# mLSTM's gate rows: loaded as rows and spread over the partitions by TensorE

## The chip, the cores and the metric

One Trainium2 chip, one of its cores. The metric is device microseconds of one execution of the whole program: two layers of a hybrid block, from the input in HBM to the normed output in HBM. The time of a kernel is the median of its runs.

## What is computed

The input has 2048 latent tokens and 256 context tokens of width 1024. Each layer projects the modulated, normed tokens to the inputs of four head groups (differential attention, HGRN2, windowed attention, mLSTM) and a gate, runs the groups, joins their outputs, and projects them back. The change lies in the mLSTM, a gated linear recurrence that runs forwards and backwards over time:

```python
logd = jnp.where(tri, cum[..., :, None] - cum[..., None, :] + ig[..., None, :], -jnp.inf)
inter = cum + m0[..., None]
m_t = jnp.maximum(jnp.max(logd, axis=-1), inter)
dmat = jnp.exp(logd - m_t[..., None])
g0 = jnp.exp(inter - m_t)
s = jnp.einsum('bhnld,bhnsd->bhnls', q, k) * dmat
num = (jnp.einsum('bhnls,bhnsv->bhnlv', s, v)
       + g0[..., None] * jnp.einsum('bhnlk,bhnkv->bhnlv', q, c0))
den = jnp.sum(s, axis=-1) + g0 * jnp.einsum('bhnlk,bhnk->bhnl', q, n0)
hid = num / jnp.maximum(jnp.abs(den), jnp.exp(-m_t))[..., None]
```

`dmat` is the causal matrix of decays of a chunk, `g0` the weight of the state that the chunk starts from. Both depend, up to a term per key, on one number per query: these are the gate rows. Four heads of width 64 each, two directions.

## The kernel before

The kernel is written in a tile framework: pools of named buffers, semaphores and the order of an engine's instructions come from its scheduler, which follows the order of the program text as far as it finds the instructions ready. Each layer has these stages. The layer's input is normed and transposed; its projections run on PE as f16 products with a high and a low part; the differential attention runs woven with the rest of the projections; then windowed attention (`swa_stream`), mLSTM (`mlstm_stream`), HGRN (`hgrn_stream`) and the output projection with the residual (`out_stream`) are woven together. They work on tiles of 128 tokens, 18 in layer 0 (16 of latent tokens and 2 of context) and 16 in layer 1, 34 in all; HGRN takes two tiles at a time.

The weave is a Python loop over generators. A stream yields its place (in tiles) and a spacing; the loop resumes the ready stream that is furthest behind. Ready is measured in PE time that the helper `mm` (the product, L94) adds up by a formula in `pe_ns`: the columns of a product, times four for f32, over 2.4 GHz. Constants in ORDER_X and ORDER_Y set the spacings. In the first phase, until the projections are through, the first tiles of windowed attention and mLSTM run beside `rest_stream`, which hands out the projections; in the second phase HGRN and the output projection join.

Helpers record the operations: L94 `mm`, L101 `tp` (transpose on PE), L105 `act` (ScalarE, ACT), L108 `tt` (tensor_tensor on VectorE, DVE, or GpSimd, POOL), L111 `stt` (DVE). Transfers are issued mostly from SyncE (SP), in program order.

Names that the change touches:

- `dr1` and `dg0`: the gate rows in HBM, per direction and tile 4 heads x 128 queries in f32, written earlier in the layer.
- `mlm`: two causal masks, 128 x 128 each, 0 or -1e30, f32. `swm`: the masks of the windowed attention and the identity, in bf16; its last part is `identb`.
- `mlstm_load(i)`: the loads of tile i. `qt`, `kt` (queries and keys), `v1` (values with a column of ones), `r1b` (the row of dr1, for two directions and four heads, repeated on all 128 partitions by a broadcast transfer, L1383), `g0b` (the rows of dg0, repeated on 64 partitions for each head of a pair, L1385), `og` (output gate, L1388). In the same function POOL multiplies g0b with qt and adds the mask to r1b, ACT takes the Exp of r1b with a bias per key (TM), DVE clamps og (L1394) and ACT takes its sigmoid. r1b, g0b and the other tiles have two buffers.
- `mlstm_stream`: at the start of tile i it calls mlstm_load(i + 1), then makes the products qk (`mqk`), DVE multiplies them onto r1b, and after a yield it makes, for each direction, `num` from g0b times the state (`cst`) and r1b times v1, with a yield after each direction.
- `bank`: hands out the PSUM banks of the tag "gp" in a ring of three, four in the second phase, to mqk, num, HGRN's gA and go, and the output's ft.

Other names in the rows: E and QQ are HGRN's decay factors and scaled queries, cm and lk their loads, yt the tile that collects the four groups' outputs, fx the output product, ph and swt the windowed attention's weights before and after a transposing transfer, ptm and pfm the projections, modps the product that makes the modulation of the layers.

Of the kernel before, what the change touches and what calls it, by code (L numbers as in the profile page):

```python
# [10 lines left out]
F32 = mybir.dt.float32  # L11
F16 = mybir.dt.float16
BF16 = mybir.dt.bfloat16
U8 = mybir.dt.uint8
AF = mybir.ActivationFunctionType
ALU = mybir.AluOpType
# [17 lines left out]
P = 128  # L34
# [19 lines left out]
M_ID, M_HG, M_SWP, M_SWN, M_MLF, M_MLB, NMASK = 0, 1, 8, 9, 10, 11, 12  # L54
# [10 lines left out]
def bc(ap, axis, n):  # L65

    a = ap.unsqueeze(axis)
    shape = list(a.shape)
    shape[axis] = n
    return a.broadcast_to(shape)  # L70
# [3 lines left out]
def kernel(  # L74
# [8 lines left out]
    V, A, G, PE, SP = nc.vector, nc.scalar, nc.gpsimd, nc.tensor, nc.sync  # L83
# [9 lines left out]
    def mm(o, lhsT, rhs, start, stop):  # L93
        PE.matmul(o, lhsT=lhsT, rhs=rhs, start=start, stop=stop)  # L94
        n = 1
        for d_ in rhs.shape[1:]:
            n *= d_
        pe_ns[0] += max(128, n * 4 if rhs.dtype == F32 else n) / 2.4
# [5 lines left out]
    def act(o, i, f, **kw):  # L104
        A.activation(out=o, in_=i, func=f, **kw)  # L105

    def tt(e, o, a, b, op):
        return e.tensor_tensor(out=o, in0=a, in1=b, op=op)  # L108
# [5 lines left out]
    ident = const.tile([P, P], F32, tag="ident", name="ident")  # L114
# [35 lines left out]
    sel = const.tile([P, 2], F32, tag="sel", name="sel")  # L150
# [108 lines left out]
    for l in range(n_layers):  # L259
# [11 lines left out]
        def dt_(name, shape, dt=F32):  # L271
            return dram.tile(shape, dt, tag=f"{name}{l}", name=f"{name}{l}")
# [16 lines left out]
        dr1 = dt_("dr1", [2, NT, 4, P])  # L289
        dg0 = dt_("dg0", [2, NT, 4, P])  # L290
        dog = dt_("dog", [T, 256])
# [6 lines left out]
        TM = lp.tile([P, 3, 2, NT * 4], F32, tag="TM", name=f"TM{l}")  # L298
# [3 lines left out]
        def jpos(d, t):  # L302

            return (t - NL if t >= NL else t + 2) if d == 0 else NT - 1 - t
# [896 lines left out]
        with ExitStack() as st4:  # L1201
            sw = st4.enter_context(tc.tile_pool(name=f"sw{l}", bufs=2, reuse_waits="tile", side="right"))
            ml = st4.enter_context(tc.tile_pool(name=f"ml{l}", bufs=2, reuse_waits="tile", side="right"))
# [9 lines left out]
            def bank(shape, name):  # L1213
                turn_[0] += 1
                if gps2 and turn_[0] % GPB == 0:
                    return gps2.tile(shape, F32, tag="gp", name=name)
                return gps.tile(shape, F32, tag="gp", name=name, bufs=GPB - 1)
# [10 lines left out]
            def room(i):  # L1228

                return lambda: i < done["out"] + (YTB if done["rest"] else 2)  # L1230
# [25 lines left out]


            mv = masks.rearrange("p (m q) -> p m q", q=P)
            mlm = ml.tile([P, 2, P], F32, tag="mlm", name="mlm", bufs=1)
            SP.dma_start(mlm, mv[:, M_MLF:M_MLF + 2])  # L1260
            swl = sw.tile([P, 640], F32, tag="sp", name="swl")[:, 0:3 * P].rearrange("p (m q) -> p m q", q=P)
            SP.dma_start(swl[:, 0:2], mv[:, M_SWP:M_SWP + 2])
            V.tensor_copy(swl[:, 2], ident)
            swm = sw.tile([P, 3, P], BF16, tag="swm", name="swm", bufs=1)
            V.tensor_copy(swm, swl)
            identb = swm[:, 2]


            KSc = sw.tile([P, 4, CTX], F16, tag="KSc", name="KSc", bufs=1)
# [98 lines left out]
            def mlstm_load(i):  # L1368
                if i >= len(order):
                    return None  # L1370
                t = order[i]
                qt_ = ml.tile([P, 2, P], F32, tag="qt", name="qt")
                SP.dma_start(qt_, dmq[:, :, t * P:(t + 1) * P].rearrange("b p t -> p b t"))
                kt_ = ml.tile([P, 2, P], F32, tag="kt", name="kt")
                SP.dma_start(kt_, dmk[:, :, t * P:(t + 1) * P].rearrange("b p t -> p b t"))
                v1 = ml.tile([P, 4, 65], F32, tag="v1", name="v1")
                SP.dma_start(v1[:, :, 0:64], dmv[t * P:(t + 1) * P].rearrange("p (h d) -> p h d", h=4))
                G.memset(v1[:, :, 64:65], 1.0)
                js = [jpos(d, t) for d in range(2)]
                r1b = ml.tile([P, 2, 4, P], F32, tag="r1b", name="r1b")  # L1380
                g0b = ml.tile([P, 2, 2, P], F32, tag="g0b", name="g0b")
                for d in range(2):
                    SP.dma_start(r1b[:, d], dr1[d, js[d]].partition_broadcast(P))  # L1383
                    for a in range(2):
                        SP.dma_start(g0b[a * 64:(a + 1) * 64, d],  # L1385
                                     dg0[d, js[d]].rearrange("(a i) q -> i a q", i=2)[a].partition_broadcast(64))
                og = ml.tile([P, 256], F32, tag="og", name="og")
                SP.dma_start(og, dog[t * P:(t + 1) * P])  # L1388
                tt(G, g0b, g0b, bc(qt_, 1, 2), ALU.mult)
                for d in range(2):  # L1390
                    tt(G, r1b[:, d], r1b[:, d], bc(mlm[:, d], 1, 4), ALU.add)
                    for h in range(4):
                        act(r1b[:, d, h], r1b[:, d, h], AF.Exp, bias=TM[:, 0, d, js[d] * 4 + h:js[d] * 4 + h + 1])
                V.tensor_scalar(og, og, ZLOW, None, ALU.max)  # L1394
                sigmoid(og, og)
                return js, qt_, kt_, v1, r1b, g0b, og

            def mlstm_stream():
                places = state_places(ml, 65, 1, "cst")
                nxt = mlstm_load(0)  # L1400
                for i in range(len(order)):
                    yield i, 0.0 if i else SW0, room(i)
                    js, qt_, kt_, v1, r1b, g0b, og = nxt
                    nxt = mlstm_load(i + 1)
                    cst = states_of(dmC, [order[i]], 65, places, i)
                    hq = yt_of(i)[:, 768:].rearrange("p (h d) -> p h d", d=64)
                    qks = [bank([P, 2, P], "mqk") for _ in range(2)]
                    for pr in range(2):
                        for pa_ in range(2):
                            r_ = slice(pa_ * 64, pa_ * 64 + 64)  # L1410
                            mm(qks[pa_][:, pr], kt_[r_, pr], qt_[r_, pr], True, True)
                    for pa_ in range(2):
                        dv = r1b.rearrange("p d (a i) q -> p d a i q", i=2)[:, :, :, pa_]
                        tt(V, dv, bc(qks[pa_], 1, 2), dv, ALU.mult)
                    yield i + 0.2, MLW, None
                    for d in range(2):
                        num = bank([P, 2, 2, 65], "mnum")
                        dn = ml.tile([P, 4], F32, tag="dn", name="dn", bufs=4)
                        for pr in range(2):
                            mm(num[:, pr].rearrange("p i c -> p (i c)"), g0b[:, d, pr], cst[:, d, pr, 0], True, False)  # L1420
                            for pa_ in range(2):
                                h = pr * 2 + pa_
                                mm(num[:, pr, pa_], r1b[:, d, h], v1[:, h], False, pa_ == 1)
                        nv = num.rearrange("p a i c -> p (a i) c")
                        act(dn, nv[:, :, 64], AF.Abs)
                        tt(V, dn, dn, TM[:, 2, d, js[d] * 4:js[d] * 4 + 4], ALU.max)
                        V.reciprocal(dn, dn)
                        hd = ml.tile([P, 4, 64], F32, tag="hd", name="hd", bufs=1) if d else hq
                        tt(V, hd, nv[:, :, 0:64], bc(dn, 2, 64), ALU.mult)
                        yield i + 0.5 + 0.4 * d, MLW, None  # L1430
                    tt(G, hq, hq, hd, ALU.add)
                    sq = ml.tile([P, 64], F32, tag="msq", name="msq", bufs=1)
                    rs = ml.tile([P, 2, 4], F32, tag="mrs", name="mrs")
                    for j in range(4):
                        act(sq, hq[:, j], AF.Square, accum_out=rs[:, 0, j:j + 1])
                    rstd_of(rs[:, 1], rs[:, 0], 64)
                    tt(V, hq, hq, bc(rs[:, 1], 2, 64), ALU.mult)
                    tt(G, hq, hq, bc(gml, 1, 4), ALU.mult)
                    hqf = hq.rearrange("p h d -> p (h d)")
                    tt(G, hqf, hqf, og, ALU.mult)  # L1440
                    done["ml"] = i + 1
# [292 lines left out]
```

## Time and profile before

| | |
|---|---|
| median of 3 runs | 4094.21 us (4089.32 to 4104.06) |
| profiled execution | 4102.18 us |
| its span, first to last instruction | 4100.4 us |
| PE busy | 3358.2 us (82%) |
| DVE busy | 2831.4 us (69%) |
| ACT busy | 2330.9 us (57%) |
| POOL busy | 2375.0 us (58%) |
| DMA, mean | 152 GB/s |

The profile is one execution. An engine is busy while one of its instructions runs; PE's ends are modelled. Idle time of an engine is put down to what ended it: "A <- B" is A waiting for B. The chain is followed back from the last instruction, at each step to what released it, or to the instruction before it on its engine. "SPq" is time in which SP issues transfers.

### The profile page before, as it was taken

How to read it: one execution, taken by the hardware profiler on the slowest of the kernel's cores; microseconds unless marked ns; L12 is line 12 of the kernel's file. 1: busy time of each engine (PE TensorE's matmuls, PEld its weight loads, DVE VectorE, ACT ScalarE, POOL GpSimd, SP SyncE). 2: the span in 40 equal slices, each digit the busy share in tenths (PEclk: the TensorE clock that was granted, in tenths of full speed). 3: DMA queues.
4: the chain of work that ended last, by engine and by line, in shares of the span. 5: the costliest groups of instructions: out<-in, count | busy, mean ns of one | idle time of the engine just before them, and what ended most of it. 6: DMA issues, size and time to landing. Idle time of an engine off the chain costs nothing. (4 is left out here: it accounts for less than half of the span.)

```text
span 4100.4 us, 77666 instructions
## 1 busy us (share of the span) xinstructions
PE 3358.2 (82%) x29798; PEld 2269.8 (55%) x29798; DVE 2831.4 (69%) x4343; ACT 2330.9 (57%) x4662; POOL 2375.0 (58%) x1701
## 2 busy tenths in 40 slices
PE   6988878888768996888888988778887698758888
PEld 4656645444546765555557466444445476545554
DVE  5158888888896647465544398988888865467665
ACT  4245655556655636566654266656666665456764
POOL 4443455443445538798966535665334564488885
PEclk8999989999989995898889999999998899869999
DMA  6356866667656628577845457667676584366783
GB/s 211 91 149 150 186 136 159 140 141 154 145 128 157 161 95 200 149 194 185 205 119 177 126 125 151 135 140 155 148 162 142 125 193 116 106 162 170 183 194 104
DMA packets 1267259, 622.12 MB, mean 152 GB/s; under 512 B 931972, under 2 KB 1214152, under 8 KB 1266888
## 3 DMA queue, kind: packets, MB, share of 16 engines
q1 hardware_dynamic: 1164520, 490.65, 53.1%
q10 hardware_dynamic: 102368, 126.52, 9.2%
q8 instruction: 234, 3.83, 0.4%
q14 instruction: 137, 1.12, 0.1%
HBM read 291.76 MB, written 131.23 MB: 103 GB/s over the span
## 5 line engine op out<-in xcount | busy, mean ns | idle before, releaser
L108 POOL TENSOR_TENSOR p<-p,p 128x1024 f16<-128x1024 f32 (+2 forms) x264 | 629.4, 2385 | 792.7 <-ACT p L1084 722.8
L105 ACT ACTIVATE p<-scr,sm 128x1024 f32<-128x1024 f32 (+2 forms) x528 | 628.3, 1194 | 417.8 <-DVE sm L1073 145.2
L94 PE MATMUL ptm<-wb,hh 128*128 128x256 f16 (+2 forms) x5024 | 835.6, 273 | 32.6 <-DVE dSs L111 7.9
L1048 DVE TENSOR_REDUCE sm<-scr 128x1 f32<-128x1024 f32 (+2 forms) x528 | 699.3, 1327 | 218.3 <-PE scr L94 214.5
L94 PE MATMUL pfm<-hh,wb 128*128 128x512 f16 (+1 forms) x2592 | 805.7, 375 | 32.7 <-DVE gz L111 10.1
L94 PE MATMUL ptm<-wb,hl 128*128 128x256 f16 (+2 forms) x2512 | 672.1, 273 | 1.7 <-POOL hl L108 1.7
L94 PEld LDWEIGHTS <-wb 128*128 128x128 f16 x3888 | 378.1, 101 | 414.3 <-issue 84.0
L94 PE MATMUL scr<-Ks,Qs 128*128 128x512 f16 (+1 forms) x1296 | 364.8, 381 | 284.5 <-ACT p L105 279.4
L94 PEld LDWEIGHTS <-hh 128*128 128x128 f16 x5024 | 480.1, 100 | 133.9 <-issue 40.0
L94 PE MATMUL pfm<-hl,wb 128*128 128x512 f16 (+1 forms) x1296 | 485.6, 375 | 0.0
L111 DVE SCALAR_TENSOR_TENSOR p<-p,sm,p 128x1024 f32<-128x1024 f32 (+2 forms) x264 | 413.8, 1568 | 8.1
L94 PEld LDWEIGHTS <-Qs 128*128 128x128 f16 x1296 | 130.7, 102 | 425.2 <-issue 354.5
L94 PE MATMUL fx<-wo,mh 128*128 128x512 f16 x1088 | 342.4, 396 | 16.8 <-DVE xt L111 8.5
L1084 ACT CAST p<-p 128x1024 f16<-128x1024 f32 (+2 forms) x264 | 297.7, 1128 | 39.2 <-DVE p L111 33.8
L94 PEld LDWEIGHTS <-wt 128*128 128x128 f16 x4640 | 243.9, 102 | 71.4 <-DMA wt<-p 24.4
L94 PE MATMUL pv<-Vs,wt 128*128 128x128 f16 (+1 forms) x4640 | 258.5, 213 | 21.9 <-DMA wt<-p 13.5
L94 PEld LDWEIGHTS <-hl 128*128 128x128 f16 x2512 | 250.8, 100 | 35.4 <-POOL hl L108 3.4
L108 POOL TENSOR_TENSOR ph<-swp,ph 128x640 f16<-128x640 f32 (+2 forms) x136 | 196.0, 1442 | 53.7 <-ACT ph L1335 44.3
L108 POOL TENSOR_TENSOR E<-lk,cm 128x512 f32<-128x512 f32 (+1 forms) x136 | 204.8, 1506 | 34.6 <-DMA cm<-dhc 17.8
L94 PE MATMUL fx<-wo,mlo 128*128 128x512 f16 x544 | 212.9, 391 | 1.4 <-DVE mlo L108 1.1
L105 ACT ACTIVATE E<-E 128x1024 f32<-128x1024 f32 x136 | 143.2, 1054 | 102.8 <-POOL E L108 98.9
L108 DVE TENSOR_TENSOR QQ<-hq,E 128x512 f32<-128x512 f32 x119 | 143.8, 1214 | 65.2 <-ACT E L105 46.7
(301 smaller groups left out, 6577.2 us busy)
## 6 DMA issues: line engine op xcount, KB each, us to landing
wraw<-in_w_in_dram SPq DMA_DIRECT2D x60, 512.0 KB
dgt<-ga ACTq DMA_DIRECT2D x68, 256.0 KB
r1b<-dr SPq DMA_DIRECT2D x68, 256.0 KB
gtt<-dgt SPq DMA_DIRECT2D x34, 512.0 KB
mraw<-in_w_mod_dram SPq DMA_DIRECT2D x64, 256.0 KB
vi<-dhi SPq DMA_DIRECT2D x49, 256.0 KB
KSb<-dsk SPq DMA_DIRECT2D x56, 192.0 KB
Ks<-dka SPq DMA_DIRECT2D x64, 144.0 KB
```

Source lines behind the costliest of these rows:

```text
L94: PE.matmul(o, lhsT=lhsT, rhs=rhs, start=start, stop=stop)
L105: A.activation(out=o, in_=i, func=f, **kw)
L108: return e.tensor_tensor(out=o, in0=a, in1=b, op=op)
L111: V.scalar_tensor_tensor(out=o, in0=a, scalar=s, in1=b, op0=op0, op1=op1)
L1048: V.tensor_reduce(sm[:, m * 2 + j:m * 2 + j + 1], ps[:, :n], AX.X, ALU.min)
L1084: A.copy(wl[:, :n], p[:, :n])
```

## The change

The gate rows are no longer broadcast by transfers. A new tile `rw` takes them as rows: the row of dr1 of each direction on one partition (0 and 32), the rows of dg0 on partitions 64 and 65. A constant `sel` holds ones on partitions 0 to 63, and on partitions 64 and 65 a pattern that picks one of two heads for each half of the 128 output partitions. A product of sel and rw puts the rows on all partitions of a PSUM bank: one f32 product of 512 columns for g0b, one per direction for r1b. The masks move into swm in bf16, and r1b's bank is opened by a bf16 product of the identity with the mask, repeated over four heads. DVE multiplies g0b's bank with qt, ACT takes the Exp from r1b's banks. All of this, and og's clamp and sigmoid, moves from mlstm_load into a new function `mlstm_rows_of`, called for the first tile ahead of its work and for each next tile after the first direction of the present one. The loads stay where they were. ORDER_X and ORDER_Y stay as they are.

```diff
             mv = masks.rearrange("p (m q) -> p m q", q=P)
-            mlm = ml.tile([P, 2, P], F32, tag="mlm", name="mlm", bufs=1)
-            SP.dma_start(mlm, mv[:, M_MLF:M_MLF + 2])
-            swl = sw.tile([P, 640], F32, tag="sp", name="swl")[:, 0:3 * P].rearrange("p (m q) -> p m q", q=P)
+            swl = sw.tile([P, 640], F32, tag="sp", name="swl").rearrange("p (m q) -> p m q", q=P)
             SP.dma_start(swl[:, 0:2], mv[:, M_SWP:M_SWP + 2])
-            V.tensor_copy(swl[:, 2], ident)
-            swm = sw.tile([P, 3, P], BF16, tag="swm", name="swm", bufs=1)
+            SP.dma_start(swl[:, 2:4], mv[:, M_MLF:M_MLF + 2])
+            V.tensor_copy(swl[:, 4], ident)
+            swm = sw.tile([P, 5, P], BF16, tag="swm", name="swm", bufs=1)
             V.tensor_copy(swm, swl)
-            identb = swm[:, 2]
+            mlm, identb = swm[:, 2:4], swm[:, 4]
+
+            sel = ml.tile([P, P], F32, tag="sel", name="sel", bufs=1)
+            V.memset(sel[0:64], 1.0)
+            V.tensor_copy(sel[64:66].rearrange("r (i c) -> r i c", c=64), bc(ident[64:66, 64:66], 2, 64))
...
                 js = [jpos(d, t) for d in range(2)]
+                rw = ml.tile([P, 512], F32, tag="rw", name="rw", bufs=1)
+                for d in range(2):
+                    SP.dma_start(rw[d * 32:d * 32 + 1], dr1[d, js[d]].rearrange("h q -> (h q)").unsqueeze(0))
+                    SP.dma_start(rw[64:66, d * 256:(d + 1) * 256].rearrange("i (a q) -> i a q", q=P),
+                                 dg0[d, js[d]].rearrange("(a i) q -> i a q", i=2))
+                og = ml.tile([P, 256], F32, tag="og", name="og")
+                SP.dma_start(og, dog[t * P:(t + 1) * P])
+                return js, qt_, kt_, v1, rw, og
+
+            def mlstm_rows_of(js, qt_, kt_, v1, rw, og):
+
                 r1b = ml.tile([P, 2, 4, P], F32, tag="r1b", name="r1b")
                 g0b = ml.tile([P, 2, 2, P], F32, tag="g0b", name="g0b")
+                gp_ = bank([P, 2, 2, P], "g0p")
+                mm(gp_.rearrange("p d a q -> p (d a q)"), sel[64:66], rw[64:66], True, True)
+                tt(V, g0b, gp_, bc(qt_, 1, 2), ALU.mult)
                 for d in range(2):
-                    SP.dma_start(r1b[:, d], dr1[d, js[d]].partition_broadcast(P))
-                    for a in range(2):
-                        SP.dma_start(g0b[a * 64:(a + 1) * 64, d],
-                                     dg0[d, js[d]].rearrange("(a i) q -> i a q", i=2)[a].partition_broadcast(64))
-                og = ml.tile([P, 256], F32, tag="og", name="og")
-                SP.dma_start(og, dog[t * P:(t + 1) * P])
-                tt(G, g0b, g0b, bc(qt_, 1, 2), ALU.mult)
-                for d in range(2):
-                    tt(G, r1b[:, d], r1b[:, d], bc(mlm[:, d], 1, 4), ALU.add)
+                    rp_ = bank([P, 4, P], "r1p")
+                    mm(rp_, identb, bc(mlm[:, d], 1, 4), True, False)
+                    mm(rp_.rearrange("p h q -> p (h q)"), sel[d * 32:d * 32 + 1], rw[d * 32:d * 32 + 1], False, True)
                     for h in range(4):
-                        act(r1b[:, d, h], r1b[:, d, h], AF.Exp, bias=TM[:, 0, d, js[d] * 4 + h:js[d] * 4 + h + 1])
+                        act(r1b[:, d, h], rp_[:, h], AF.Exp, bias=TM[:, 0, d, js[d] * 4 + h:js[d] * 4 + h + 1])
                 V.tensor_scalar(og, og, ZLOW, None, ALU.max)
                 sigmoid(og, og)
                 return js, qt_, kt_, v1, r1b, g0b, og
...
                     yield i, 0.0 if i else SW0, room(i)
+                    if i == 0:
+                        nxt = mlstm_rows_of(*nxt)
                     js, qt_, kt_, v1, r1b, g0b, og = nxt
                     nxt = mlstm_load(i + 1)
...
                         yield i + 0.5 + 0.4 * d, MLW, None
+                        if d == 0 and nxt:
+                            nxt = mlstm_rows_of(*nxt)
                     tt(G, hq, hq, hd, ALU.add)
```

## Rows read from the trace of the kernel before

**Rows 1.** The page's slices, 40 of 102.5 us: busy tenths, then granted clock.

```profile
PE   6988878888768996888888988778887698758888
POOL 4443455443445538798966535665334564488885
PEclk8999989999989995898889999999998899869999
```

**Rows 2.** Stretches: length, busy us of each engine (instructions), granted clock, DMA share, GB/s.

```profile
core 0: us, PE busy (x) PEld busy (x) DVE busy (x) ACT busy (x) POOL busy (x), PEclk, DMA share, GB/s
1291.00:1560.00 269.00, 243.63 (x2032) 182.92 (x2030) 140.09 (x269) 136.27 (x294) 132.03 (x120) 0.95 0.52 141
1560.00:2130.00 570.00, 466.19 (x4857) 326.46 (x4856) 337.21 (x587) 359.76 (x972) 488.17 (x387) 0.83 0.72 178
3280.00:3560.00 280.00, 243.32 (x2042) 181.15 (x2040) 162.89 (x279) 155.95 (x319) 144.40 (x121) 0.94 0.52 133
3560.00:4060.00 500.00, 398.40 (x4415) 273.34 (x4414) 333.08 (x550) 315.84 (x855) 425.30 (x339) 0.87 0.69 172
```

**Rows 3.** Tile r1b: count, ns min/median/max, starts, forms; then idle before, us, times.

```profile
L105 ACT ACTIVATE r1b<-r1b,TM x272: 385/392/417, 1297.5 to 4003.5; 128x128 f32<-128x128 f32 x136
...
L108 POOL TENSOR_TENSOR r1b<-r1b,mlm x68: 1261/1272/2262, 1296.2 to 3997.7; 128x512 f32<-128x512 f32 x68
L108 DVE TENSOR_TENSOR r1b<-mqk,r1b x68: 653/682/693, 1301.1 to 4034.9; 128x512 f32<-128x512 f32 x68
...
  DMA r1b<-dr: 50.7, 24
```

**Rows 4.** Tile g0b, the same view.

```profile
L108 POOL TENSOR_TENSOR g0b<-g0b,qt x34: 1259/1272/2253, 1300.0 to 4000.3; 128x512 f32<-128x512 f32 x34
```

**Rows 5.** Stretches, instructions on g0b alone: PE, PEld and POOL busy.

```profile
1560.00:2130.00 570.00, 29.37 (x116) 20.54 (x116) 19.71 (x14) 0.83 0.72 178
...
3560.00:4060.00 500.00, 23.49 (x104) 18.04 (x104) 16.80 (x12) 0.87 0.69 172
```

**Rows 6.** Waits, whole span: engine, line, waited for, us, times, longest.

```profile
ACT E L105 <- POOL E L108: 98.9, 55, 8.1
...
PEld L94 <- DMA swt<-ph: 75.2, 40, 5.0
...
ACT og L105 <- DVE og L1394: 64.9, 26, 9.2
DVE og L1394 <- DMA og<-dog: 64.5, 23, 5.7
...
PE gA L94 <- DVE QQ L108: 48.7, 25, 7.8
...
DVE QQ L108 <- ACT E L105: 46.7, 37, 4.5
```

**Rows 7.** Chain that ended last, 3560 to 4101 us: shares of that stretch.

```profile
by line: POOL E L108 14.5%; PE fx L94 10.9%; issue 9.0%; POOL yt L108 8.7%; POOL ph L108 4.2%; DMA cm<-dhc 4.0%; DMA g0b<-dg 3.4%; POOL r1b L108 2.4%; SPq L1385 2.2%; DMA swt<-ph 2.0%; PE go L94 1.9%; DMA gtt<-dgt 1.9%; POOL g0b L108 1.7%; 
```

**Rows 8.** PE by shape: tile modps; then the costliest groups with fx.

```profile
L94 PE MATMUL modps<-mraw,sc x384: 379/403/637, 11.9 to 739.1; 128*32 128x256 f32 x192
...
L94 PE MATMUL fx<-wo,mh 128*128 128x512 f16 x1088 | 342.4, 396 | 16.8 <-DVE xt L111 8.5 <-DVE yt L108 5.8 <-ACT mh L1600 2.5
```

**Rows 9.** PE in order of time: start us, length us, instructions.

```profile
1791.58 0.60 PE L94 MATMUL fx<-wo,mh 128*128 128x512 f16 x2
1792.01 0.38 PE L94 MATMUL fx<-wo,mlo 128*128 128x512 f16 x1
1792.22 0.59 PE L94 MATMUL fx<-wo,mh 128*128 128x512 f16 x2
```

## Prediction

> **What bounds the kernel now.** I read the page first: its slices put the mLSTM in two places, near the end of each layer, and PE, POOL and the granted clock differ from slice to slice there [rows 1]. So no share of the whole span says what an edit in the mLSTM is worth. The stretches do [rows 2]. In each layer the mLSTM runs through two phases. In the first one (1291 to 1560 us and 3280 to 3560 us) the rest of the projections is woven with the first tiles: PE is busy for 243.6 of 269 us and 243.3 of 280 us, POOL for half. In the second (1560 to 2130 us and 3560 to 4060 us) HGRN and the output projection join: POOL is busy for 488 of 570 us (86%) and 425 of 500 us (85%), PE for 466 (82%) and 398 (80%), at a granted clock of 0.83 and 0.87 against 0.95 and 0.94 in the first. The change takes work from the busiest engine of the second phase and gives work to the busiest one of the first.
>
> Next the two tiles that the change touches. POOL makes 68 additions for r1b and 34 products for g0b, 1.26 to 1.27 us each at the median [rows 3, 4]. Ahead of the additions POOL stood idle for 50.7 us in 24 waits for the transfer into r1b [rows 3]: an engine that takes its instructions in order holds up everything behind that addition, the E of HGRN above all. The same shape is seen at og: DVE waits 64.5 us for its transfer and ACT 64.9 us for DVE [rows 6], because the load and its first reader are issued together. Who waits for POOL in its turn: ACT for E 98.9 us, then DVE for ACT's E 46.7 us, then PE for QQ 48.7 us [rows 6]. Last the chain that ended last, which covers layer 1's second phase to the end of the program, 3560 to 4101 us, 541 us long [rows 7]. The operations that the change removes stand on it: landing of g0b 3.4% (18.4 us), r1b additions 2.4% (13.0 us), g0b products 1.7% (9.2 us), the issuing of g0b's transfers on SP 2.2% (11.9 us). PE's output product has 10.9% and its other named line 1.9%.
>
> **POOL and transfers, what goes.** All 102 POOL instructions go (102 x 1.27 = 130 us), and so do two broadcast transfers of 256 KB and four of 64 KB per tile, replaced by four small ones (two rows of 2 KB, two pairs of rows of 2 KB a pair). SP issues four where it issued six, so of g0b's 11.9 us on the chain half stays, since two of its four issues remain. In layer 1 that is 18.4 + 13.0 + 9.2 + 6.0 = 46.6 us of chain. It is an upper bound, because when it goes the next chain beside it is late: E, yt and ph on POOL itself hold 27.4% of the chain and stay [rows 7]. The lower bound is nothing at all. I take half, 23.3 us: POOL at 85% has other work that then runs earlier, but PE, at 80%, isn't far behind. Layer 0 has no chain in the profile; its second phase has 14 of these tiles against 12 [rows 5], so I take 27.2 us. Together -50.5 us, between 0 and -101.
>
> The readers move too: g0b, the Exp of r1b and og's sigmoid are now issued half a tile (some 17 us, 570 us over 16 tiles, halved) after their loads. The waits for og on DVE and ACT should go; they are idle time of engines that are 59% to 67% busy, so of 64.5 us I count a tenth, -6 us, between 0 and -20. The small transfers have the same 17 us to land in, so I cost PE's wait for them at nothing; the cover is the half tile, and if it were gone a wait would cost PE what POOL paid, 50.7 us over 24 waits, 2.1 us each. The new rows have one buffer: SP's load for the next tile waits until this tile's products have read it, and all loads behind it on SP (og, cst and the other streams') wait with it. Those products lie half a tile before that load, so nothing again; without that cover SP would stand for the pitch of the products, 1.3 us a tile.
>
> **PE, what comes.** Each tile adds one f32 product of 512 columns for g0b, two for r1b, and two bf16 products of 512 columns for the mask. No row shows an f32 product 512 wide, nor one over one or two rows at this width. The nearest are the modulation's, 256 columns f32: 379 ns at the least, 403 at the median, against 396 ns for 512 columns f16 [rows 8]. A record of half the columns is as long, so an f32 column costs about two f16 columns. Back to back, two f16 products of 512 columns start 0.43 us before the next one, 0.215 us each [rows 9]. A tile then costs 3 x 0.43 + 2 x 0.215 = 1.72 us at this clock. From below the bound is one f16 column per f32 column, 5 x 0.215 = 1.08 us; from above a product occupies PE for twice the modulation's whole record, 2 x 0.403 us: 3 x 0.81 + 0.43 = 2.86 us. I take 1.72, since the modulation's row is the nearest.
>
> The Trainium skill's page "FP8 and Floating Point Precision" (TensorE Precision Notes) says that true FP32 takes four passes through the array. The row above looks like two, and no run here shows these very products. By four passes of 512 columns the added work would be 3 x 0.86 + 0.43 = 3.01 us a tile, an estimate from that page and the f16 pitch; it stands close to the upper bound, and rival E is what it would do.
>
> In the second phase 26 tiles [rows 5] x 1.72 = 44.7 us come to an engine that is idle for 104 of 570 us and 102 of 500 us; at three tenths (the chain shows PE's two large lines at 12.8%, and smaller ones besides) that is +13.4 us, between 6 (12.8%) and 74 (26 x 2.86, all of it). In the first phase the other 8 of 34 tiles x 1.72 = 13.8 us lie on an engine that is 90% busy: at nine tenths +12.4 us, between 0 and 24.
>
> **DVE, ACT, banks.** DVE takes over the g0b product, from PSUM. The nearest row is r1b times qk, also 128x512 with one operand in PSUM: 682 ns [rows 3]. 34 x 0.68 = 23 us on an engine 59% to 67% busy: +2 us, between 0 and 23. ACT's eight Exp per tile (392 ns each [rows 3]) stay, only their source is PSUM: nothing, since they are as many and as wide.
> Three PSUM banks more are taken per tile from a ring of three, four in the second phase, that the qk, num, gA, go and ft products share. A bank of r1b is held until its four Exp are done, 4 x 0.39 = 1.6 us plus ACT's queue; what is queued behind on PE is everything, the next gA first. Price 0 to 8 x 0.39 = 3.1 us per tile, 0 to 82 us in all. I take 0.2 us, +5 us: the ring serves some 17 banks a tile, in 34 us, so a hold of 2 us usually ends before its turn.
>
> **The sum.** -50.5 - 6 + 13.4 + 12.4 + 2 + 5 = -23.7 us against the profiled execution of 4102.2 us (span 4100.4): 4078.5. The median of the three runs is 4094.2, 8 us lower, so 4070.
>
> **The rivals.**
> A. PE takes POOL's place as the bound, and the result is slower. Place: the second phase. For it: POOL's load goes to PE where PE is already at 80%, and PE's own waits for swt (75.2 us [rows 6]) end with a transfer, not with POOL. It decides when PE's idle time doesn't shrink, so that all the new work lengthens the phase: 26 x 1.72 + 12.4 = +57, less a quarter of the chain's gain (25) = +32 us, 4126. Against it: 48.7 us of PE's waits, those for QQ, lead back to E on POOL [rows 6]. 0.18.
> B. The banks. PE stands behind r1b's Exp: at 1.5 us a tile, 39 us in place of 5: 4104; at 2.5 us 4130. It decides above 1.1 us a tile, where the sum turns positive. 0.09.
> C. Nothing: POOL's gaps fill with waits for ACT (ph, E) and the chain goes on through fx and yt. Gains and costs of some 30 us cancel: 4094. 0.16.
> D. The clock rises. With PE waiting less, the granted clock of the second phase goes from 0.85 to the first phase's 0.94 [rows 2]: 865 us of PE busy time shrink by a tenth, some 82 us, three tenths of it on the path: -25; with three quarters of the chain's gain in place of half, another -25: 4020 to 4045. For it: PE is then busier. 0.15.
> E. The f32 products cost the upper bound, 1.14 us more a tile: 26 x 1.14 x 0.3 + 8 x 1.14 x 0.9 = +17 us: 4087, no change that can be told. 0.05: only the row's whole length as pitch speaks for it.
>
> **How the numbers follow.** The forecast, 4070, has 0.37. Times can be told apart here from about 0.3%, 12 us. Faster: the forecast and D, 0.52, and a little of C and E, 0.54. Slower: A and most of B, 0.26. Same: the rest, 0.20. Range 4005 to 4130: it reaches into D's lower end and A's 4126.
>
> **What would show it.** Right: in the second phases POOL busy falls from 86% and 85% to some 76%, PE rises to 84% or more, no wait of POOL for r1b, DVE's and ACT's waits for og nearly gone, r1p and g0p products at pitches near 0.43 us. Wrong: PE idle before gA or num with nothing but a bank to wait for; phases as long as before while POOL is idle; f32 products twice as long; or an order of the streams so different (the weave goes by the PE time that the helper on L94 adds up, by whose formula a tile has 3 x 853 + 2 x 213 ns = 3 us more) that phases shift by more than these terms.

## The result, and the profile after

The change makes the kernel slower: 4154.9 us in the median of four runs (4150.8 to 4164.4), beside 4094.3 us of the kernel before, in four runs too (4089.3 to 4104.1), a ratio of 1.0148 with a 95% interval from 1.0122 to 1.0174. The forecast was 4070 us with a range up to 4130: wrong in sign, and the time is outside the range. The profiled execution took 4164.4 us, its span is 4162.7 us, 62 us longer than before.

The page's slices, 40 of 104.1 us, of the changed kernel (compare [rows 1]):

```profile
PE   6988878888769987999989887787877787779998
...
POOL 4443455443444437778757545645334543666764
PEclk9999999999989996889899999999998888779999
```

POOL's digits in the mLSTM's places fell (8 7 9 8 9 became 7 7 7 8 7, and 8 8 8 8 5 at the end became 6 6 7 6 4), and PE's rose to 9. The stretches of the changed kernel, the two phases of each layer, cut about where the phases now end; columns as in [rows 2]:

```profile
1291.00:1570.00 279.00, 258.42 (x2018) 183.47 (x2015) 131.60 (x269) 132.41 (x287) 114.81 (x106) 0.92 0.45 123
1570.00:2150.00 580.00, 535.66 (x5086) 351.18 (x5085) 338.47 (x618) 366.51 (x987) 429.08 (x349) 0.85 0.64 157
3290.00:3600.00 310.00, 268.65 (x2077) 191.87 (x2075) 165.32 (x289) 160.95 (x323) 130.92 (x112) 0.89 0.43 113
3600.00:4120.00 520.00, 450.59 (x4462) 292.99 (x4462) 325.56 (x554) 308.62 (x836) 358.18 (x295) 0.86 0.58 143
```

In the second phases POOL went from 86% and 85% to 74% (429 of 580) and 69%, and PE from 82% and 80% to 92% (536 of 580) and 87%. PE is now the busiest engine there by far. Its own waits say the same: its wait for swt was 75.2 us and its wait for QQ 48.7 us [rows 6]; here the same lines read

```profile
PEld L94 <- DMA swt<-ph: 24.1, 18, 4.6
...
PE gA L94 <- DVE QQ L108: 15.2, 9, 3.8
```

So what used to stop PE is earlier, as intended, and PE is late all the same. The tiles of the new products, r1p (two banks of r1b) and then g0p (the bank of g0b); columns as in [rows 3]:

```profile
L105 ACT ACTIVATE r1b<-r1p,TM x272: 347/367/407, 1302.8 to 4084.4; 128x128 f32<-128x128 f32 x136
L94 PEld LDWEIGHTS r1p<-rw,sel x136: 181/184/333, 1301.6 to 4081.7; 1*128 1x128 f32 x136
L94 PE MATMUL r1p<-rw,sel x136: 587/692/1217, 1301.6 to 4082.6; 1*128 1x512 f32 x136
L94 PE MATMUL r1p<-swm x68: 379/390/634, 1301.3 to 4081.0; 128*128 128x512 bf16 x68
```

```profile
L94 PE MATMUL g0p<-rw,sel x68: 587/692/1217, 1300.3 to 4076.9; 2*128 2x512 f32 x68
L108 DVE TENSOR_TENSOR g0b<-g0p,qt x34: 677/684/693, 1301.4 to 4079.5; 128x512 f32<-128x512 f32 x34
```

Two things are to be seen. The count: 34 tiles make 68 products r1p and 34 products g0p, but there are 136 and 68 records. Each f32 product is two records. The length: a record takes 692 ns at the median and up to 1217 ns, where a bf16 product of as many columns takes 390. The chain from 3560 us to the end, which here begins 40 us ahead of layer 1's second phase, has lost the lines that the change removed [rows 7], and PE's lines fill it: fx 15.3% where it had 10.9%, r1p 5.0%:

```profile
by line: PE fx L94 15.3%; POOL E L108 6.8%; issue 6.7%; POOL yt L108 6.2%; PE r1p L94 5.0%; PE mnum L94 3.5%; PE gA L94 3.5%; DMA og<-dog 3.4%; DVE xt L111 3.3%; DMA braw<-in_w_out_dram 2.9%; PE ptm L94 2.7%; DVE QQ L108 2.5%; PE ss L94 2.4
```

### The profile page after: what moved, and what is told of

Read it like the earlier page. It is cut to its first block, busy times and chain, and to the rows that moved or that the text cites. A ratio compares the mean times of both kernels' runs of the same rounds, so it can differ in the third digit from the quotient of the medians.

```text
span 4162.7 us, 78158 instructions
## 1 busy us (share of the span) xinstructions
PE 3512.9 (84%) x30070; PEld 2318.2 (56%) x30070; DVE 2815.0 (68%) x4381; ACT 2330.3 (56%) x4662; POOL 2221.8 (53%) x1599
## 5 line engine op out<-in xcount | busy, mean ns | idle before, releaser
L94 PE MATMUL pv<-Vs,wt 128*128 128x128 f16 (+1 forms) x4640 | 255.5, 212 | 25.8 <-DMA wt<-p 15.3
L108 POOL TENSOR_TENSOR ph<-swp,ph 128x640 f16<-128x640 f32 (+2 forms) x136 | 186.2, 1369 | 140.8 <-ACT ph L1338 104.9
L108 DVE TENSOR_TENSOR rp<-rp,cs 128x512 f32<-128x512 f32 (+1 forms) x64 | 80.0, 1253 | 135.6 <-POOL rt L108 122.1
```

## Experiments

The question is where the gain went. The theory after this profile: the removal is worth what was forecast, but the products cost far more PE time than 1.72 us a tile. The rivals: the moved readers and small loads, the order of the streams, the banks. All ratios are to the kernel before, run beside each kernel on the same chip, with 95% intervals. The code cuts are shortened; `...` stands for what is left out.

| kernel | median, us | ratio, interval |
|---|---|---|
| the change | 4154.9 | 1.0148 [1.0122, 1.0174] |
| e1, one-pass products in place of f32 | 4064.1 | 0.9919 [0.9894, 0.9943] |
| e2, rows as two f16 parts | 4069.3 | 0.9926 [0.9901, 0.9951] |
| e3, f32 products over 128 rows | 4113.0 | 1.0034 [1.0019, 1.0049] |
| e4, before with late readers | 4099.5 | 1.0004 [0.9986, 1.0023] |
| e5, before with the change's PE count | 4091.4 | 0.9991 [0.9978, 1.0004] |
| e6, f16 parts over 128 rows | 4059.0 | 0.9918 [0.9903, 0.9933] |
| e7, before without POOL's 102 instructions | 4067.3 | 0.9931 [0.9912, 0.9949] |
| e8, before without the gate rows | 4028.9 | 0.9839 [0.9810, 0.9868] |
| e9, e6 with two row tiles | 4048.9 | 0.9885 [0.9863, 0.9906] |
| e10, e6 with three og tiles | 4063.2 | 0.9910 [0.9886, 0.9935] |
| e11, e6 once more | 4059.9 | 0.9905 [0.9879, 0.9930] |

**e1: the products in one pass.** The stand-ins read constants of 128 rows; the count that orders the streams is kept by adding what f32 would have counted.

```diff
-mm(gp_..., sel[64:66], rw[64:66], True, True)
+mm(gp_..., identb, bc(identb, 1, 4), True, True); pe_ns[0] += 640.0
-mm(rp_..., sel[d * 32:d * 32 + 1], rw[d * 32:d * 32 + 1], False, True)
+mm(rp_, identb, bc(low, 1, 4), False, True); pe_ns[0] += 640.0
```

> The changed kernel with each of the three f32 spreading products of a tile replaced by a one-pass bf16 product of the same 512 columns on constant data, so r1b and g0b no longer hold the gate rows; loads, banks, readers and the PE time that the weave counts stay as in the changed kernel. Theory P (the f32 products cost PE some 4 us a tile and PE became the bound of the second phases): 3 x 0.7 to 0.8 us a tile leave PE, 75 to 100 us in all, and the time falls from 4155 to 4085 to 4115. Theory O (the order of the streams, the moved readers and the longer held banks cost it): all of that is still there, 4140 to 4160. Theory K (products over one or two rows let the granted clock fall): they are gone too, so it falls as with P, but the clock of the second phases rises from 0.85 and 0.86 to 0.90 or more.

Measured: 0.9919. With the banks, the moved readers, the loads and the mask products all in place, but the three f32 products cheap, the change is faster than before, and below theory P's range of 4085 to 4115. Its second phases are granted 0.89 and 0.91, so P and K are both open still. So the loss is in those three products, by their type, their rows or both.

**e2: the same result from f16 rows.** The rows are stored as a high and a low f16 part, so that one f16 product over two or four rows adds them up.

```diff
-SP.dma_start(rw[d * 32:d * 32 + 1], dr1[d, js[d]]...)
+SP.dma_start(rw[d * 32:d * 32 + 2], dr1[:, d, js[d]]...)
-mm(rp_..., sel[d * 32:d * 32 + 1], rw[d * 32:d * 32 + 1], False, True)
+mm(rp_..., sel[d * 32:d * 32 + 2], rw[d * 32:d * 32 + 2], False, True)
```

> The gate rows are stored as a high and a low f16 part and spread by one f16 product over two or four rows each, in place of f32 products; the mask product stays; the weave's count of PE time falls by 1.9 us a tile with them. Theory P: PE has 5 one-pass products a tile, some 1.5 us with their weight loads, against 4; 4080 to 4115, about the kernel before or a little below. Theory O: 4135 to 4160. Theory K: the products still have two and four rows, so the clock stays as in the changed kernel, 0.85 and 0.86, and the time stays above 4120.

Measured: 0.9926, as e1, and here with the right rows. The stand-ins of e1 were a fair measure. It is below theory P's range, and theory K's, above 4120, failed: the second phases are granted 0.89 and 0.89.

**e3: the same f32 products, contracted over all 128 rows.** rw is filled with zeros once, and the weights, now zero outside the rows that they pick, leave the others out.

```diff
+V.memset(rw, 0.0)
-mm(gp_..., sel[64:66], rw[64:66], True, True)
+mm(gp_..., sel, rw, True, True)
-mm(rp_..., sel[d * 32:d * 32 + 1], rw[d * 32:d * 32 + 1], False, True)
+mm(rp_..., bc(ident[:, d * 32], 1, P), rw, False, True)
```

> The changed kernel with the same f32 products contracted over all 128 rows, the unused rows being zero. Theory K: the granted clock of the second phases rises from 0.85 and 0.86 to 0.90 or more, the f32 records at half clock become fewer, and 15 to 40 us come back: 4115 to 4140. Theory P and theory O: neither passes nor columns change, 4145 to 4165.

Measured: 1.0034, where the change has 1.0148. The columns, the type, the transfers and the count are the same; only the rows that take part, 128 with zeros in most, differ. The tile r1p of e3, then its stretches (the same phases):

```profile
L94 PE MATMUL r1p<-rw,ident x136: 590/592/593, 1302.8 to 4030.9; 128*128 128x512 f32 x136
L94 PE MATMUL r1p<-swm x68: 376/379/390, 1302.6 to 4030.2; 128*128 128x512 bf16 x68
```

```profile
1565.00:2132.00 567.00, 501.05 (x5112) 334.16 (x5112) 341.28 (x615) 362.03 (x985) 429.53 (x347) 0.92 0.65 161
...
3570.00:4090.00 520.00, 441.43 (x4538) 296.50 (x4539) 325.02 (x557) 312.57 (x855) 359.35 (x301) 0.89 0.59 145
```

No record of r1p is long any more (in the change 31 of 136 are over 700 ns), and the granted clock of the second phases is 0.92 and 0.89 in place of 0.85 and 0.86. One tile in order of time shows how. PE in the changed kernel (start us, length us), then the weight loads around the first three of these products, then the clock of the stretches around it:

```profile
1895.86 1.12 PE L94 MATMUL g0p<-rw,sel 2*128 2x512 f32 x2
1896.91 0.39 PE L94 MATMUL r1p<-swm 128*128 128x512 bf16 x1
1897.24 1.12 PE L94 MATMUL r1p<-rw,sel 1*128 1x512 f32 x2
1898.29 0.60 PE L94 MATMUL fx<-wo,mh 128*128 128x512 f16 x2
1898.73 0.38 PE L94 MATMUL fx<-wo,mlo 128*128 128x512 f16 x1
1898.95 0.38 PE L94 MATMUL r1p<-swm 128*128 128x512 bf16 x1
1899.26 1.41 PE L94 MATMUL r1p<-rw,sel 1*128 1x512 f32 x2
1900.60 0.80 PE L94 MATMUL mnum<-cst,g0b 128*128 128x130 f32 x2
```

```profile
1895.86 0.29 PEld L94 LDWEIGHTS g0p<-rw,sel 2*128 2x128 f32 x2 [0.42 <-DMA gtt<-dgt]
1896.91 0.10 PEld L94 LDWEIGHTS <-swm 128*128 128x128 bf16 x1 [0.76 <-issue]
1897.23 0.29 PEld L94 LDWEIGHTS r1p<-rw,sel 1*128 1x128 f32 x2 [0.23 <-issue]
```

```profile
1885.00:1895.80 10.80, 10.08 (x122) 1.00 0.61 158
1895.80:1898.20 2.40, 2.40 (x6) 1.00 1.11 240
1898.20:1901.20 3.00, 3.00 (x10) 0.79 0.62 127
1901.20:1905.00 3.80, 3.80 (x49) 0.50 1.02 176
1905.00:1915.00 10.00, 10.00 (x113) 0.91 0.58 160
```

The same views of e3:

```profile
1898.78 1.02 PE L94 MATMUL g0p<-rw,sel 128*128 128x512 f32 x2
1899.64 0.38 PE L94 MATMUL r1p<-swm 128*128 128x512 bf16 x1
1899.86 1.02 PE L94 MATMUL r1p<-rw,ident 128*128 128x512 f32 x2
...
1902.87 0.39 PE L94 MATMUL mnum<-cst,g0b 128*128 128x130 f32 x2
```

```profile
1898.57 0.41 PEld L94 LDWEIGHTS g0p<-rw,sel 128*128 128x128 f32 x2
1899.21 0.10 PEld L94 LDWEIGHTS <-swm 128*128 128x128 bf16 x1 [0.24 <-issue]
1899.64 0.41 PEld L94 LDWEIGHTS r1p<-rw,ident 128*128 128x128 f32 x2 [0.33 <-issue]
```

```profile
1888.70:1898.70 10.00, 10.00 (x122) 1.00 1.07 262
1898.70:1901.00 2.30, 2.30 (x13) 1.00 0.02 1
1901.00:1903.00 2.00, 2.00 (x21) 1.00 0.00 0
```

In e3 the f32 product holds PE for 0.86 us (1898.78 to 1899.64), and the weights of the next product are loaded 0.2 to 0.4 us ahead (1899.21 for the product at 1899.64). In the change the product holds PE for 1.05 us at the same granted clock of 1.00 (1895.86 to 1896.91): weight loads and products start at the same moment, so nothing is loaded ahead of a product whose rows differ from those of the one before it. Then the clock falls while PE is busy all the time: 0.79, and 0.50 (1.2 GHz) for the 3.8 us behind the last product, so that mnum, which has nothing to do with the change, takes 0.80 us where the same two instructions take 0.39 us in e3 at 1902.87.

The other tiles show the same. In the 10 us from the first of a tile's products the granted clock, averaged over the 34 tiles, is 0.79 in the change, and under 1.00 in 26 of them; in e3 it is 0.99, and under 1.00 in 6. So theory K holds for the f32 products.

The Trainium skill's page "TensorEngine Tiling (Array Packing)", Key Properties, says that a change of tiling mode drains TensorE. The weight loads above, which start 0.07 us before the end of the product before them and not earlier, fit that if products over one or two rows and over 128 count as two modes; no run here shows the mode.

**e4 and e5: the kernel before with one side effect alone.** e4 moves the readers of r1b, g0b and og half a tile later, on their old engines, with the old transfers. e5 adds to the count of PE time what the change adds, so that the streams are resumed in the change's order.

```diff
 # e4
+def mlstm_rows_of(...):  # POOL, ACT, DVE readers, called as in the change
 # e5, after the first direction's yield
+if d == 0 and nxt: pe_ns[0] += 2987.0
```

> The kernel before with its broadcast transfers and POOL instructions, but the readers of r1b, g0b and og moved half a tile behind their loads, as the change does. Theory P: the moves alone are a gain or nothing, since POOL, DVE and ACT lose their waits for r1b and og (50, 64 and 65 us of idle time): 4070 to 4100. Theory O: the move is part of the loss: 4110 to 4150.

> The kernel before, and nothing added but the count: the weave's sum of PE time grows by 2987 ns at the place where the change puts its products, so the streams are asked for in the order that the count gives. Theory O: a good part of the 60 us comes back here, 4115 to 4150. Theories P and K: 4085 to 4110.

Measured: 1.0004 and 0.9991, neither told from no change. In e4 the waits got shorter, but stayed (whole span, columns as in [rows 6]):

```profile
DVE og L1398 <- DMA og<-dog: 43.3, 18, 6.0
POOL r1b L108 <- DMA r1b<-dr: 40.4, 17, 5.9
```

**e6: f16 parts over 128 rows.** e2 with the zero-filled tile of e3.

> The f16 rows of the second run, contracted over all 128 rows with zeros in the unused ones. Theory K: a product over two or four rows costs clock whatever its type, if less of it with one pass; the granted clock of the second phases rises from 0.89 to 0.91 or more and the time falls below the second run's 4069, to 4045 to 4062. If rows matter only for long f32 products: 4060 to 4080.

Measured: 0.9918, and 0.9905 when run again (e11). The first two of a tile's five products in order of time, and what follows the fifth:

```profile
1880.23 0.38 PE L94 MATMUL g0p<-rw,sel 128*128 128x512 f16 x1
1880.45 0.38 PE L94 MATMUL r1p<-swm 128*128 128x512 bf16 x1
...
1881.31 0.39 PE L94 MATMUL mnum<-cst,g0b 128*128 128x130 f32 x2
```

1.08 us a tile, 0.215 us each, at full clock. Against e2 (two and four rows, 0.9926) the intervals overlap, so the time doesn't say whether a narrow contraction costs something in one pass too. The traces say what it costs PE: at full clock each of the five products of a tile holds PE for 0.32 us in e2 and for 0.22 us in e6, and in e2 too no weights are loaded ahead. They also say that the clock doesn't fall behind these products: in the 10 us from the first of them it is 0.94 in e2 and 0.94 in e6, and in the second phases 0.89 and 0.89 against 0.90 and 0.89. So theory K isn't borne out for one pass.

**e7 and e8: what the removal is worth.** e7 is the kernel before without POOL's 102 instructions; e8 also without the broadcast transfers.

```diff
 # e7
-tt(G, g0b, g0b, bc(qt_, 1, 2), ALU.mult)
-tt(G, r1b[:, d], r1b[:, d], bc(mlm[:, d], 1, 4), ALU.add)
-act(r1b[:, d, h], r1b[:, d, h], AF.Exp, ...)
+act(r1b[:, d, h], r1b[:, d, h], AF.Identity, ...)
 # e8, besides
-SP.dma_start(r1b[:, d], ...); SP.dma_start(g0b[...], ...)
-act(r1b[:, d, h], r1b[:, d, h], AF.Identity, ...)
+act(r1b[:, d, h], ident, AF.Identity, ...)
-mm(num..., g0b[:, d, pr], cst..., True, False)
+mm(num..., qt_[:, pr], cst..., True, False)
```

> The kernel before without POOL's 102 instructions on r1b and g0b (the mask and the queries are left out, and ACT makes Identity in place of Exp); transfers, ACT and DVE instructions stay. The sum of the prediction takes half of what POOL and the transfers hold on the chain; POOL's own half of it is some 25 us: 4065 to 4080. If POOL at 86% was the bound of the second phases, 4 us a tile fall out almost whole there: 3990 to 4030.

> As the run before, and the broadcast transfers of r1b and g0b left out too (ACT reads the identity, the state product reads the queries). This is all that the change removes, with nothing put in its place. By the sum of the prediction -51 us against the kernel before: 4035 to 4060. If half of the chain was too little: 3960 to 4020. If the transfers don't matter: the same as the run before.

Measured: 0.9931 (-28 us, -36 to -21) and 0.9839 (-66 us, -78 to -54). The removal is worth what was forecast and a little more. POOL's instructions are 28 us of it, and the transfers, taken out after them, the other 38 +- 14; which part is the larger the intervals don't tell. The second phases of e8:

```profile
1560.00:2110.00 550.00, 466.58 (x4961) 317.43 (x4959) 336.64 (x598) 362.10 (x974) 434.17 (x345) 0.90 0.68 168
...
3520.00:4000.00 480.00, 390.40 (x4369) 269.54 (x4370) 327.38 (x540) 308.54 (x849) 369.80 (x299) 0.88 0.66 156
```

The clock is 0.90 and 0.88 there, where it was 0.83 and 0.87 [rows 2]: a clear rise in layer 0 alone.

**e9, e10, e11: the waits that are left, in e6.** e9 has two row tiles in turn, e10 three og tiles, e11 is e6 again on their chip.

```diff
 # e9
+rw = rws[i % 2]
 # e10
+og = ml.tile([P, 256], F32, tag="og", name="og", bufs=3)
```

> The f16 rows over all 128 rows, with two row tiles taken in turn in place of one, so that SP's load of the next rows no longer waits until PE has read these (24.9 us of SP's waits in that run). If that wait holds up what is queued behind it on SP: 4035 to 4052 against 4059. If SP has room for it: 4052 to 4065.

> The same f16 rows with one row tile, and three buffers for og in place of two, so that its load doesn't wait for POOL's last product of the tile but one. The waits of DVE for og and of ACT for DVE (45 and 47 us with the f16 rows over few rows) should go; if idle time of DVE and ACT counts: 4035 to 4052, if not 4052 to 4065.

> The f16 rows over all 128 rows once more, beside the two: 4052 to 4066 by the first time, 4059.

Measured: 0.9885, 0.9910 and 0.9905. e9 has the lowest median, 4048.9 us, and is faster than both kernels; its interval overlaps that of e11, so the second tile itself is not shown to help. Nor does SP's wait ahead of the row load show it: in e6, with one tile, then in e9, with two,

```profile
SPq L1394 <- PE r1p L94: 24.9, 11, 4.9
```

```profile
SPq L1396 <- PE r1p L94: 26.1, 10, 4.7
```

What holds SP there stays open. The third og tile didn't change the time. DVE's wait for og is shorter with it, but stays (35.0 us in 19 waits in e10, 48.0 us in 26 in e6).

## Why the prediction was wrong, step by step

The runs split the change into steps, each the difference of two ratios times 4094 us; the uncertainty joins the half-widths of the two intervals by the root of their squares.

| step | runs | us |
|---|---|---|
| all that the gate rows cost before goes | before to e8 | -66 +- 12 |
| products of one pass, masks, DVE's product, banks, loads come | e8 to e1 | +33 +- 16 |
| f32 in place of one pass | e1 to e3 | +47 +- 12 |
| one or two rows in place of 128 | e3 to the change | +47 +- 12 |

**What goes** was sized well in the sum: 50.5 and 6 forecast, 66 measured. That half of the chain's share would come true was a choice, and that it came close is one case, not a rule. The 6 us for og and the late readers are not in it: e4 shows nothing, and in the change the wait of ACT for og is 59.3 us (64.9 before), that of DVE 41.0 (64.5). "Should go" was wrong: a reader half a tile later still waits for this transfer; why it lands so late stays open.

**The step that failed is the price of PE's products, 1.72 us a tile.** It rested on the modulation's row [rows 8]: 403 ns for 256 f32 columns, 396 ns for 512 f16 columns, "so an f32 column costs about two f16 columns". That compared records, not products. In the kernel, `mod_half` makes four such products for one modps tile; the timeline of the kernel before has eight records there:

```profile
264.31 0.64 PE L94 MATMUL modps<-mraw,sc 128*32 128x256 f32 x8
```

There are two records for each product. (The x192 at the end of the row in [rows 8] is not the number of products: in [rows 3] ACT's 272 Exp, eight a tile, have x136 there.) Two records worth two f16 columns each make four f16 columns for an f32 column, 4 x 0.215 = 0.86 us for 512. e3 shows just that, 0.86 us from start to start. A tile is then 3 x 0.86 + 2 x 0.215 = 3.0 us. The upper bound, 2.86, came near, but it was said that "only the row's whole length as pitch" speaks for it, and it got 0.05. The kernel's own formula in `mm` spoke for it too: four columns for an f32 column, 853 ns a product, as the prediction's last paragraph has it.

The Trainium skill's page "FP8 and Floating Point Precision", TensorE Precision Notes, with its four passes for FP32 gave 3.01 us a tile, and e3's trace agrees; the prediction set the misread row against it.

**The second half of the same term** is that the products of the change cost more than 3.0: from 1895.86 to 1900.60 the g0p product, the two masks and the two r1p products hold PE for 1.05 + 0.33 + 1.05 + 0.31 + 1.34 = 4.08 us. Over all 34 tiles these five products hold it, from start to start, for 146 us in the change and for 105 in e3, 4.3 and 3.1 us a tile. The prediction noted that no row showed a product over one or two rows, and then took the price of 128 rows without a bound for it. The span of the change is 50 us longer than that of e3, and PE is busy for 92 us more in it (3512.9 against 3420.4). Two estimates, which overlap, cover these 92. PE is busy at half clock for 572 us in the change and for 424 in e3; half of the 148 more, 74 us, is time that full clock would have saved. And weights that aren't loaded ahead cost 3 x 0.2 + 2 x 0.1 = 0.8 us a tile (1.05 against 0.86, 0.33 against 0.215), 27 us.

**The share of PE's time that reaches the end** was three tenths in the second phases and nine tenths in the first, 0.44 over all 34 tiles. From e1 to e3 a tile has 3 x (0.86 - 0.215) = 1.94 us more, 66 us over 34 tiles, and the time grows by 47: 0.7. Once POOL's work has gone, PE's work counts for more than the chain before the change, where PE's lines had a small share, could tell. With the right price and the share as forecast the sum would be -23.7 + 34 x 0.44 x (3.0 - 1.72) = -5 us, no change. With 0.7 for all of PE's products it is -23.7 - 13.4 - 12.4 + 0.7 x 34 x 3.0 = +22, where e3 has +14 (1.0034), and with the change's 4.3 us it is +53, where 61 was measured. The 0.7 is itself taken from these runs, so this shows that the terms fit together, not that they were to be known.

**Rivals.** A, PE takes POOL's place and the result is slower, came nearest, though not by its own condition: PE's idle time did shrink, from 205 to 114 us in the two second phases, while PE's busy time grew by 122. Its 4126 used 1.72 too, and with 3.0 it would have been 26 x 3.0 + 8 x 3.0 x 0.9 - 25 = +75, 4169 where 4155 was measured; but the change's products cost 4.3, so that this comes near is luck. E had nearly the price over 128 rows, but neither the share nor the narrow products. D, the clock rises, is right in part: without the narrow products the second phases are granted 0.88 to 0.92 (e3, e8) in place of 0.83 and 0.87, and the change, at 0.85 and 0.86, loses most of that. B, the banks: the waits of PE in the change show none for r1b's Exp or for g0b's product, and e1 has all the banks and is faster than before. C, nothing, is refuted by e8.

**Small steps.** DVE's product took 684 ns (682 forecast). ACT's Exp from PSUM took 367 ns against 392. POOL fell to 74% and 69% (some 76% forecast), and its additions onto r1b, with their waits, are gone. The order of the streams, named as what could upset the sum, is worth nothing that can be told (e5; e1 has the change's order too). That the single row tile costs nothing is open: SP waits 40.8 us in 11 waits ahead of that load in the change, but two tiles didn't shorten such a wait (e9).

## What to carry to other kernels

Count the records of a product before pricing it from one: set the records of a stretch of the timeline against the products that the program makes there. And price by the time from start to start, not by the length of a record. To spread rows over the partitions, use parts of 16 bits in one pass and let the contraction run over all 128 rows of a zero-filled tile, which in one pass saves PE 0.1 us a product, though no time that can be told (e2, e6); here that turned +1.5% into -0.8% (e6; -1.2% in e9, which isn't told from it). Work that was moved to an engine at 80% was paid here at 0.7 of its length (e1 to e3), where the chain before the move had led to 0.44.

## What the runs showed of the hardware

An f32 product of 512 columns is two records and holds TensorE for 0.86 us at full clock, four times the 0.215 us of an f16 one. A product over one or two rows, for the same columns, takes 1.05 us at the same granted clock, with no weights loaded ahead of it or of the product behind it, and the granted clock falls behind a few of them although PE has no gap: 1.00, 0.79, 0.50 in stretches of 2.4, 3.0 and 3.8 us. Over 128 rows, all but four of them zeros, it stays at 1.00 around the products shown (e3). The few rows and the missing load ahead don't lower it by themselves: e2's f16 products have both, and its clock behind them is that of e6, 0.94. The f32 products over few rows do; what in them does it stays open.
